# Up projections of a block as seven block products per pair of chunks, with split weights kept in HBM

## The chip, the cores and the metric

The kernel runs on one core of a Trainium2 chip. The metric is the device time of one execution in microseconds (us), the median of several runs.

## What is computed

The reference is one inference step of a one-layer decoder trunk on 2064 prompt rows (16 learned ones and 2048) and 64 sample rows (8 sequences of 8), all in float32, D = 1024 and F = 2816. Cut to what matters:

```
z = rmsnorm(x) @ w_in                                # 1024 -> 5120, five branches
a = silu(layernorm(dwconv31(za * sigmoid(zg)))) @ w_conv_out
p = (multiscale_pool(zp) @ w_pool) * pool_scale
x = x + (sigmoid(gate_a) * a + sigmoid(gate_b) * p) @ w_out
up = dwconv3(rmsnorm(x) @ w_up)                      # 1024 -> 2 x 2816
v, g = up[:F], up[F:]
x = x + (gelu(g) * v) @ w_down                       # 2816 -> 1024
y = rmsnorm(x)
```

The last rows before each convolution and pool are outputs too.

## The kernel before

The rows lie on the free axis, the channels on the 128 partitions, in chunks of 128 channels: 8 for D, 22 for F. The 2128 rows go in three blocks (708, 708 and 712 columns; the last holds the 64 sample rows at its end), and each block in two column tiles of half its width, since a PSUM region takes 512 columns.

**Products.** Every float32 operand is held as a rounded part (hi) and the rest (lo), and each product is three matmuls: lo times hi, hi times lo, hi times hi (`gemm`, matmuls at line 200). A unit is one chunk of output channels: up projections take 8 contraction chunks x 2 column tiles x 3 = 48 matmuls into one PSUM buffer of two regions. There are four such buffers in turn. `join` lets the first three units of some stages run together, chunk by chunk, as their operands appear.

**Weights.** `w_loads` fetches a unit's float32 weights (512 KB) into one of two raw tiles; `w_split` rounds them on ScalarE (line 183) and takes the rest on VectorE (line 167), into one of four places. Weights are read and split anew for each block and column tile: 416 times.

**Work beside the products.** Each unit has a post-processing step (`post`). For the up projections (`v_post`, `g_post`, `up_conv`) ScalarE scales by the last tap, VectorE adds the two other taps (line 171) and handles the sample rows apart (three small steps); the gate half then has a Gelu on ScalarE, the product with the value half on VectorE, the rounding on ScalarE and the rest on VectorE. Norms, convolution and pooling are tasks written as generators.

**Order.** One Python loop writes the instructions: it goes through the units, and after each one lets `drip` write steps of posts, weight splits and tasks, in this order of urgency, until VectorE's forecast time (`Pace`, a table of costs) is near that of TensorE. Each engine then runs its own list in order and waits by semaphores. All DMAs go through one queue, SP's, in the order written.

**Feed-forward of a block** (`FF`). Value and gate chunk f in turn, each its own unit. After a group of chunks the down projection over this group (`DN`: 8 units, each adds its result to x) is put behind the first up projections of the next group. The last block has groups of 8, 7 and 7, its first units and its last down projection go by column tile, and x stays in SBUF (`add_post`).

Of the kernel before, what the change touches and what calls it, by code (L numbers as in the profile page):

```python
# [14 lines left out]
P = 128  # L15
D = 1024
KC = D // P
F = 2816
# [33 lines left out]
RAW_BUFS = 2  # L52
F_GROUPS = (6, 5, 5, 6)
# [8 lines left out]
LAST_GROUPS = (8, 7, 7)  # L62
OWN = 4
POOL_ORDER = (1, 0, 3, 2)
BOTH, FIRST, SECOND = (0, 1), (0,), (1,)
# [3 lines left out]
class Pace:  # L69
    """A rough forecast of when each engine gets to an instruction; it only orders the work between engines."""  # L70
# [30 lines left out]
    def alloc(self, tag, bufs, ap):  # L101
        """A tile of a rotating pool waits for the last use of the tile that had its place."""
# [9 lines left out]
class Unit:  # L112
    def __init__(self, w, mm, post, needs, wait):
        self.w, self.mm, self.post, self.needs, self.wait = w, mm, post, needs, wait
        self.joined = False
# [8 lines left out]
def trunk(ctx: ExitStack, tc: tile.TileContext, A, O):  # L124
# [4 lines left out]
    mpool = ctx.enter_context(tc.tile_pool(name="mpool", bufs=2))  # L129
    ppool = ctx.enter_context(tc.tile_pool(name="ppool", bufs=4, space=bass.MemoryType.PSUM))  # L130
# [16 lines left out]
    def room(k):  # L147
        """Waits until k more tiles fit, beside a few for the work that can't wait."""
# [50 lines left out]
    def mm(out, lhsT, rhs, start, stop, rate=1.0):  # L199
        nc.tensor.matmul(out, lhsT=lhsT, rhs=rhs, start=start, stop=stop)  # L200
        pace.put("pe", size(out) * rate / 2.4 + 2.5, [out], [lhsT, rhs])
# [21 lines left out]
    def sb(ap, b, ts_):  # L223
        """The columns of a tile that belong to the column tiles ts_, in the shape of ps_of."""
# [9 lines left out]
    wq = []  # L234
    wsplits = {}
    wstate = {"load": 0, "split": 0, "done": 0}

    def w_loads():
        while wstate["load"] < min(len(wq), wstate["done"] + RAW_BUFS):
            src, n = wq[wstate["load"]][:2]  # L240
            raw = pace.alloc("raw", RAW_BUFS, wpool.tile([P, n], F32, tag="raw", name=nm("raw"), bufs=RAW_BUFS))
            load(raw, src)
            wq[wstate["load"]].append(raw)
            wstate["load"] += 1

    def w_split(i):
        while len(wq[i]) < 3:
            yield "cond", lambda: len(wq[i]) > 2
        n, raw = wq[i][1], wq[i][2]
        wh = pace.alloc("wh", W_BUFS, wpool.tile([P, n], F32R, tag="wh", name=nm("wh")))  # L250
        wl = pace.alloc("wl", W_BUFS, wpool.tile([P, n], F32R, tag="wl", name=nm("wl")))
        wq[i].append((wh, wl))
        yield "at", max(pace.ready(wh), pace.ready(raw))
        act(wh, raw, AF.Copy)
        yield at(wh)
        tt(wl, raw, wh.bitcast(F32), ALU.subtract)
        wstate["done"] += 1
        w_loads()

    def w_start(first):  # L260
        w_loads()
# [5 lines left out]
    def w_ahead(i, first):  # L267
        """Weights up to number i are split when this returns; more are under way, first is the oldest still in use."""
# [10 lines left out]
    def gemm(ps, w, pairs, rng, woff=0):  # L279
        """Products of float32 operands held as two parts each; the product of the two small parts is below float32."""  # L280
        wh, wl = w
        last = len(pairs) - 1
        for k, (xh, xl) in enumerate(pairs):
            w0 = woff + k * P
            for i, (c0, c1) in enumerate(rng):
                o = ps[:, i, : c1 - c0]
                mm(o, wl[:, w0 : w0 + P], xh[:, c0:c1], k == 0, False)
                mm(o, wh[:, w0 : w0 + P], xl[:, c0:c1], False, False)
                mm(o, wh[:, w0 : w0 + P], xh[:, c0:c1], False, k == last)
# [990 lines left out]
```

## Time and profile before

| what | value |
|---|---|
| median of 3 runs | 3006.57 us (3005.26 to 3006.57) |
| span of the profiled execution | 3004.0 us |
| TensorE busy | 2963.5 us, 18156 instructions |
| VectorE busy | 2162.5 us |
| ScalarE busy | 970.3 us |
| read from and written to HBM | 236.09 and 12.75 MB |

The page gives for the profiled execution the span from its first to its last instruction; the median lies 2.6 us above it. A row of a group reads: line, engine, operation, output<-inputs, shapes, count | busy us, mean ns of one | idle us of the engine just before, and what ended most of it. A row of waits reads: who waited <- for whom: us in total, times, longest us. A row of the timeline reads: start us, duration us, engine, line, operation, and in brackets the idle time before. A row of a stretch reads: from:to and its length, then the busy us (and the number of instructions) of PE, PEld, DVE, ACT and POOL, the granted clock, the DMA engines' busy share (of one, or of the stretch's us in its length) and GB/s; where only PE was asked for, its busy us stands alone. PE is TensorE, DVE VectorE, ACT ScalarE, SP the engine that issues the DMAs.

### The profile page before, as it was taken

How to read it: one execution, taken by the hardware profiler on the slowest of the kernel's cores; microseconds unless marked ns; L12 is line 12 of the kernel's file. 1: busy time of each engine (PE TensorE's matmuls, PEld its weight loads, DVE VectorE, ACT ScalarE, POOL GpSimd, SP SyncE). 2: the span in 40 equal slices, each digit the busy share in tenths (PEclk: the TensorE clock that was granted, in tenths of full speed). 3: DMA queues.
4: the chain of work that ended last, by engine and by line, in shares of the span. 5: the costliest groups of instructions: out<-in, count | busy, mean ns of one | idle time of the engine just before them, and what ended most of it. 6: DMA issues, size and time to landing. Idle time of an engine off the chain costs nothing.

```text
span 3004.0 us, 43514 instructions
## 1 busy us (share of the span) xinstructions
PE 2963.5 (99%) x18156; PEld 2956.5 (98%) x18156; DVE 2162.5 (72%) x2958; ACT 970.3 (32%) x1311; POOL 87.9 (3%) x185
## 2 busy tenths in 40 slices
PE   7999999999999999999999999999999999999998
PEld 7999999999999999999999999999999999999998
DVE  7999998789899856633698899986763366535356
ACT  4212234343222333522332322333352244313132
POOL 0111000010000000000010000000000000000000
PEclk9999999999999999999999999999999999999999
DMA  4211221422221223123332122222322242222223
GB/s 166 75 36 60 71 70 47 156 80 60 74 71 55 79 86 119 64 78 117 122 99 68 61 80 65 66 74 75 122 86 77 96 137 74 79 68 77 71 77 114
DMA packets 95235, 251.64 MB, mean 84 GB/s; under 512 B 22080, under 2 KB 30400, under 8 KB 95040
## 3 DMA queue, kind: packets, MB, share of 16 engines
q1 hardware_dynamic: 95040, 248.88, 25.4%
q8 instruction: 142, 2.33, 0.3%
q14 instruction: 53, 0.43, 0.0%
HBM read 236.09 MB, written 12.75 MB: 83 GB/s over the span
## 4 chain that ended last, share of the span: by engine, by line
PE 97%; DVE 2%; ACT 1%; issue 0%; DMA 0%; SPq 0%; DVEq 0%; ACTq 0%
PE ps L200 97%; DVE s L171 1%; ACT s L183 1%; DVE s L167 1%; DMA s<-in_x 0%; DVE rs L171 0%; DVE wl L167 0%; ACT wh L183 0%; DVE rs L167 0%; SPq L192 0%; DVE rs L179 0%; DVE uw L167 0%; DVE rs L177 0%; DVEq L1258 0%; ACTq L183 0%
## 5 line engine op out<-in xcount | busy, mean ns | idle before, releaser
L200 PE MATMUL ps<-s,wh 128*128 128x354 f32 (+2 forms) x11904 | 2907.9, 326 | 8.0 <-DVE s L167 7.9
L200 PEld LDWEIGHTS ps<-s,wh 128*128 128x128 f32 x11904 | 2097.9, 189 | 10.7 <-DVE s L167 10.4
L200 PE MATMUL ps<-s,wl 128*128 128x356 f32 (+2 forms) x5952 | 1944.6, 327 | 6.8 <-ACT s L183 3.7
L200 PEld LDWEIGHTS ps<-s,wl 128*128 128x128 f32 x5952 | 1122.8, 189 | 8.9 <-ACT s L183 7.3
L171 DVE SCALAR_TENSOR_TENSOR s<-s,half,s 128x708 f32<-128x708 f32 (+1 forms) x720 | 626.7, 928 | 0.0
L167 DVE TENSOR_TENSOR wl<-raw,wh 128x1024 fp32r<-128x1024 f32 (+4 forms) x416 | 476.6, 1147 | 193.2 <-ACT wh L183 190.3
L183 ACT ACTIVATE wh<-raw 128x1024 fp32r<-128x1024 f32 (+4 forms) x416 | 412.3, 994 | 550.6 <-PE ps L200 410.5
L183 ACT ACTIVATE s<-s 128x708 fp32r<-128x708 f32 (+7 forms) x424 | 296.7, 710 | 548.0 <-DVE s L171 397.1
L167 DVE TENSOR_TENSOR s<-s,s 128x708 f32<-128x708 f32 (+7 forms) x453 | 358.5, 801 | 93.6 <-ACT s L183 89.4
L171 DVE SCALAR_TENSOR_TENSOR s<-ps,cst,s 128x708 f32<-128x708 f32 (+3 forms) x276 | 254.6, 924 | 189.4 <-ACT sf L183 109.7
L183 ACT ACTIVATE s<-ps,cst 128x708 f32<-128x708 f32 (+3 forms) x138 | 113.5, 825 | 457.6 <-PE ps L200 457.6
L167 DVE TENSOR_TENSOR s<-s,ps 128x708 f32<-128x708 f32 (+3 forms) x160 | 123.1, 779 | 144.9 <-PE ps L200 144.1
L183 ACT ACTIVATE s<-ps 128x708 f32<-128x708 f32 (+3 forms) x121 | 82.5, 690 | 396.4 <-PE ps L200 396.3
L171 DVE SCALAR_TENSOR_TENSOR s<-s,s 128x708 f32<-128x708 f32 (+2 forms) x96 | 85.3, 891 | 44.0 <-ACT s L183 42.4
L171 DVE SCALAR_TENSOR_TENSOR s<-s,ps 128x708 f32<-128x708 f32 (+5 forms) x65 | 44.0, 698 | 91.2 <-PE ps L200 90.5
L171 DVE SCALAR_TENSOR_TENSOR s<-s,cst,s 128x708 f32<-128x708 f32 (+3 forms) x112 | 83.5, 767 | 27.9 <-ACT s L183 14.8
L167 DVE TENSOR_TENSOR s<-s 128x722 f32<-128x722 f32 (+7 forms) x60 | 53.2, 886 | 17.0 <-ACT s L183 15.6
L171 DVE SCALAR_TENSOR_TENSOR sc<-sa,cst,sc 128x64 f32<-128x64 f32 x232 | 47.1, 278 | 0.3
L183 ACT ACTIVATE s<-s,half 128x708 f32<-128x708 f32 (+1 forms) x48 | 46.5, 975 | 0.8
L188 POOL COPY s<-phist 128x15 f32<-128x15 f32 x24 | 12.8, 534 | 1014.8 <-ACT s L183 1007.3
L188 POOL CAST s<-hhist 128x2 fp32r<-128x2 f32 x48 | 19.2, 416 | 642.9 <-PE ps L200 555.3
L200 PEld LDWEIGHTS ps<-ones,s 128*128 128x128 f32 x144 | 18.6, 197 | 11.8 <-issue 11.7
(43 smaller groups left out, 273.4 us busy)
## 6 DMA issues: line engine op xcount, KB each, us to landing
raw<-in_w_up SPq DMA_DIRECT2D x132, 512.0 KB, 3.3
raw<-in_w_in SPq DMA_DIRECT2D x112, 512.0 KB, 3.3
raw<-in_w_out SPq DMA_DIRECT2D x40, 512.0 KB, 3.3
s<-in_x SPq DMA_DIRECT2D x40, 354.0 KB, 6.1
raw<-in_w_co SPq DMA_DIRECT2D x24, 512.0 KB, 3.3
raw<-in_w_dn SPq DMA_DIRECT2D x32, 384.0 KB, 3.1
s<-in_x SPq DMA_DIRECT2D x32, 356.0 KB, 5.9
raw<-in_w_dn SPq DMA_DIRECT2D x24, 448.0 KB, 3.4
```

The costliest lines, as they stand in the source:

```text
L167: nc.vector.tensor_tensor(out=out, in0=a, in1=b, op=op)
L171: nc.vector.scalar_tensor_tensor(out=out, in0=a, scalar=s, in1=b, op0=op0, op1=op1)
L183: nc.scalar.activation(out, a, func, **kw)
L188: nc.gpsimd.tensor_copy(out, a)
L200: nc.tensor.matmul(out, lhsT=lhsT, rhs=rhs, start=start, stop=stop)
```

## The change

**Seven products.** For chunks 2 to 21 of the last block, `pair(b, f)` replaces the units of value chunk f and gate chunk f. The two chunks, the two halves of the contraction (chunks 0 to 3 and 4 to 7) and the two column tiles make a 2 x 2 by 2 x 2 block product. Eight block products become seven, of 4 contraction chunks x 3 = 12 matmuls of 358 columns each. They go into four PSUM regions x, a, bb and d of two buffers: first x, second a, third bb, fourth onto x, fifth onto bb, sixth d, seventh onto a. ScalarE copies the first results of x, a and bb (`copy`) before the fourth, seventh and fifth product add to these regions, and copies x again after the fourth. VectorE makes the outputs by five additions of 358 columns (`after`); then `v_post` and `g_post` follow as before, from SBUF.

```diff
+            x, a, bb, d = ps1[:, 0, :n], ps1[:, 1, :n], ps2[:, 0, :n], ps2[:, 1, :n]
+            prod(x, 0, 0, b11, True)
+            c1 = copy(pq[:, :n], x)
+            yield
+            prod(a, 1, 0, mx[1], True)
+            c5 = copy(pq[:, n:], a)
+            yield
+            prod(bb, 2, 0, mx[3], True)
+            for t in older:
+                done(t)
+            pu = S(2 * n)
+            c7 = copy(pu[:, :n], bb)
+            yield
+            done(c1)
+            prod(x, 0, h, b21, False)
+            w_start(w[1])
+            uv = S(2 * n)
...
+            done(c7)
+            prod(bb, 1, h, mx[4], False)
+            w_start(w[3])
+            yield
+            prod(d, 3, 0, mx[2], True)
+            yield
+            done(c5)
...
+            prod(a, 3, h, b22, False)
+            w_start(w[3] + 1)
```

`older` are the posts that are unfinished when the pair begins; all of them are written out ahead of c7. `mixed_rows` makes the combined inputs once (four rounds, each with four subtractions of 358 columns, two roundings and two rests of 716); `first_mixed` keeps the float32 rows for it. `mixed_weights`, the last of all tasks, makes the combined weights of each pair from block 1 on: one load of value and gate chunk, four combinations and seven parts of 512 columns, each rounded, its rest taken, and both stored in HBM.

```diff
+            x0, x1 = R["xt", b][k], R["xt", b][k + KC // 2]
...
+            tt(t1, b12, b11, ALU.subtract)
+            tt(t2, b22, t1, ALU.subtract)
+            tt(t3, b22, b12, ALU.subtract)
+            tt(t4, b21, t2, ALU.subtract)
```

**Weights kept.** A weight that comes again is stored in HBM as hi and lo after its first split (1 MB), and later loaded so, with no split: 136 splits remain (40 of w_in, 8 of w_co, 8 of w_out, 44 of w_up, 4 of w_pool, 32 of w_down).

```diff
+            q.both = pace.alloc("wb", W_BUFS, wpool.tile([P, 2, q.n], F32R, tag="wb", name=nm("wb")))
+            if q.known:
+                load(q.both.bitcast(F32), known(q.key))
...
+        if q.again:
+            stores.append(i)
```

**Groups and x of the last block.** The groups are 2, 5, 5, 5 and 5 chunks in place of 8, 7 and 7. x is stored in HBM after the second norm, and each down projection but the last loads a chunk, adds and stores it again; `x_back` loads it for the last.

```diff
+PLAIN = 2
+MIX_GROUPS = (2, 5, 5, 5, 5)
...
-LAST_GROUPS = (8, 7, 7)
...
                     yield from add_post(b, c, ts_, ps, "x2n" if f1 == FC else None)
+                    if f1 < FC and b in MIXED:
+                        spill(b, c)
...
+                if b in MIXED and f >= PLAIN:
+                    pair(b, f)
```

**How instructions move.** ScalarE, up projections of the last block, before: value chunk (ps_23743), gate chunk (ps_23816), and the splits (wh) between; the last two rows are Gelu and rounding.

```order
L183 ACTIVATE s_23867<-ps_23743,cst 128x712
L183 ACTIVATE sf_23741<-ps_23743 128x8x8
L183 ACTIVATE wh_23792<-raw_23739 128x1024
L183 ACTIVATE uhist<-ps_23743 128x2
L183 ACTIVATE s_23934<-ps_23816,cst 128x712
L183 ACTIVATE sf_23814<-ps_23816 128x8x8
L183 ACTIVATE wh_23865<-raw_23809 128x1024
L183 ACTIVATE uhist<-ps_23816 128x2
L183 ACTIVATE s_23934<-s_23934 128x712
L183 ACTIVATE s_23935<-s_23867 128x712
```

ScalarE, the same place now: the post of one pair (s_22983 and s_23032 are its value and gate rows), then the copies of the next pair, whose buffers are ps_23038 (x and a) and ps_23039 (bb and d).

```order
L194 ACTIVATE s_23054<-s_22983,cst 128x712
L194 ACTIVATE sf_22899<-s_22983 128x8x8
L194 ACTIVATE uhist<-s_22983 128x2
L194 ACTIVATE s_23076<-s_23032,cst 128x712
L194 ACTIVATE sf_23015<-s_23032 128x8x8
L194 ACTIVATE uhist<-s_23032 128x2
L194 ACTIVATE s_23076<-s_23076 128x712
L194 ACTIVATE s_23077<-s_23054 128x712
L194 ACTIVATE s_23040<-ps_23038 128x358 x2
L194 ACTIVATE s_23104<-ps_23039 128x358
L194 ACTIVATE s_23120<-ps_23038 128x358
```

The splits are gone, four copies from PSUM have come, and the copies of x and a (s_23040) stand behind the Gelu and the rounding of the pair before.

TensorE, before, from one up projection to the next; the new buffer is waited for, and nothing inside a unit.

```order
L200 MATMUL ps_23743<-s_21468,wh_23512 128x358
L200 MATMUL ps_23743<-s_21467,wh_23512 128x358
L200 MATMUL ps_23816<-s_21319,wl_23586 128x358 [waits DVE_49,PE_49,Activation_49]
L200 MATMUL ps_23816<-s_21320,wh_23585 128x358
L200 MATMUL ps_23816<-s_21319,wh_23585 128x358
```

TensorE now, in the pair of ps_23038 and ps_23039: the end of the third product, the fourth onto x, and the start of the fifth onto bb.

```order
L211 MATMUL ps_23039<-s_22360,wb_23000 128x358
L211 MATMUL ps_23039<-s_22359,wb_23000 128x358
L211 MATMUL ps_23038<-s_21781,wb_22981 128x358 [waits Activation_49]
L211 MATMUL ps_23038<-s_21781,wb_22981 128x358 x2
L211 MATMUL ps_23038<-s_21789,wb_22981 128x358 x3
L211 MATMUL ps_23038<-s_21824,wb_22981 128x358 x3
L211 MATMUL ps_23038<-s_21833,wb_22981 128x358 x3
L211 MATMUL ps_23039<-s_22166,wb_22998 128x358 [waits Activation_49]
```

Inside a pair there are now waits for ScalarE, at the fourth and fifth product (and the seventh).

SP, before, in the last block: a load of weights for a down projection, sample rows in, sample rows out.

```order
L192 DMA raw_25259<-in_w_dn 128x896
L192 DMA sf_25261<-in_st_ffn 128x80
L196 DMA out_ffn_s<-sf_25194 128x80
L192 DMA raw_25329<-in_w_dn 128x896
L192 DMA sf_25334<-in_st_ffn 128x80
L196 DMA out_ffn_s<-sf_25261 128x80
```

SP now, in the first down projection of the last block: xd is x in HBM, wb the weights, keep their place in HBM.

```order
L207 DMA out_ffn_s<-sf_22452 128x80
L203 DMA s_22500<-xd_0_21998 128x712
L203 DMA wb_22515<-keep_6635 128x2x256
L203 DMA s_22517<-xd_1_22014 128x712
L203 DMA wb_22532<-keep_6684 128x2x256
L207 DMA xd_0_21998<-s_22500 128x712
L203 DMA s_22536<-xd_2_22022 128x712
L203 DMA wb_22551<-keep_6733 128x2x256
L207 DMA xd_1_22014<-s_22517 128x712
L203 DMA s_22555<-xd_3_22039 128x712
```

Between two loads of weights stand a fetch and a spill of x, and from the third fetch on each one stands behind the spill of two chunks before, which waits for that chunk's addition.

More of the change, by code (lines that the diff above doesn't have):

```diff
@@ L234, in trunk @@
     wq = []
+    kept = {}
+    stores = []
     wsplits = {}
-    wstate = {"load": 0, "split": 0, "done": 0}
-    def w_loads():
[L239 to L243, printed above, removed]
+    wstate = {"load": 0, "split": 0, "done": 0, "raws": 0, "first": 0}
@@ new lines, in known, with keep @@
+    def known(key):
+        if key[0] != "dn":
+            return kept.get(key)
+        _, c, f0, f1 = key
+        done = kept.get(("dn", c), (None, ()))
+        return done[0][:, :, f0 * P : f1 * P] if all(f in done[1] for f in range(f0, f1)) else None
+    def keep(key, n):
+        if key[0] == "dn":
+            _, c, f0, f1 = key
+            if ("dn", c) not in kept:
+                kept["dn", c] = dpool.tile([P, 2, F], F32, tag=f"keep_{len(kept)}", name=f"keep_{len(kept)}"), set()
+            kept["dn", c][1].update(range(f0, f1))
+            return known(key)
+        kept[key] = dpool.tile([P, 2, n], F32, tag=f"keep_{len(kept)}", name=f"keep_{len(kept)}")
+        return kept[key]
@@ new lines, in w_stores @@
+    def w_stores(upto):
+        while stores and stores[0] <= upto:
+            q = wq[stores.pop(0)]
+            store(keep(q.key, q.n), q.both.bitcast(F32))
+    def w_loads():
+        while wstate["load"] < min(len(wq), wstate["first"] + LEAD):
+            q = wq[wstate["load"]]
+            q.known = known(q.key) is not None
+            if not q.known and wstate["raws"] >= wstate["done"] + RAW_BUFS:
+                break
+            w_stores(wstate["load"] - W_BUFS)
+            q.both = pace.alloc("wb", W_BUFS, wpool.tile([P, 2, q.n], F32R, tag="wb", name=nm("wb")))
+            if q.known:
+                load(q.both.bitcast(F32), known(q.key))
+            else:
+                q.raw = pace.alloc("raw", RAW_BUFS, wpool.tile([P, q.n], F32, tag="raw", name=nm("raw"), bufs=RAW_BUFS))
+                load(q.raw, q.src)
+                wstate["raws"] += 1
@@ L244, in w_loads @@
             wstate["load"] += 1
     def w_split(i):
[L247 to L256, printed above, removed]
+        q = wq[i]
@@ L692, in co_post, with spill, fetch, x_back @@
         R.setdefault(("m", b), []).append((hi, lo))
+    def spill(b, c):
+        if ("xd", b, c) not in R:
+            R["xd", b, c] = dpool.tile([P, WIDTHS[b]], F32, tag=f"xd_{b}_{c}", name=f"xd_{b}_{c}")
+        store(R["xd", b, c], R.pop(("x1", b, c)))
+    def fetch(b, c):
+        x = R["x1", b, c] = S(WIDTHS[b])
+        load(x, R["xd", b, c])
+    def x_back(b):
+        for c in range(KC):
+            yield from room(1)
+            fetch(b, c)
     def x_again(b):
```

250 lines of the change are left out of this document (221 added, 29 removed).

## Prediction

> **What bounds the kernel now.** I read the page first: busy times, then the chain that ended last.
>
> ```profile
> span 3004.0 us, 43514 instructions
> PE 2963.5 (99%) x18156; PEld 2956.5 (98%) x18156; DVE 2162.5 (72%) x2958; ACT 970.3 (32%) x1311; POOL 87.9 (3%) x185
> PE 97%; DVE 2%; ACT 1%; issue 0%; DMA 0%; SPq 0%; DVEq 0%; ACTq 0%
> ```
>
> TensorE is busy 99% of the span and carries 97% of the chain. Time can be won only by giving it fewer matmuls, and is lost wherever it is made to wait. So the second view is TensorE's own waits, the third its busy time by stretch, in the up projections of the last block.
>
> ```profile
> PE ps L200 <- DVE s L167: 19.3, 7, 9.6
> PE ps L200 <- DVE rs L171: 7.1, 5, 2.0
> PE ps L200 <- ACT s L183: 3.7, 3, 1.8
> PE ps L200 <- DVE s L171: 3.0, 4, 1.1
> 2600.00:2700.00 100.00, 100.00 (x615) 100.00 (x614) 39.72 (x50) 23.56 (x33) 0.00 (x0) 1.00 0.24 73
> 2700.00:2800.00 100.00, 100.00 (x611) 100.00 (x610) 58.62 (x87) 34.12 (x59) 0.00 (x0) 1.00 0.25 73
> ```
>
> All waits together are 33 us, none longer than 9.6. In the stretch that the change rewrites TensorE never waits; 1226 matmuls in 200 us are 163.1 ns each. There every new wait costs its full length.
>
> **Matmuls removed.** A pair of chunks took 2 x 8 x 2 x 3 = 96 matmuls, 15.66 us. Seven products of 4 x 3 take 84, 13.70 us. Twenty pairs: 240 x 163.1 ns = 39.1 us less. A product is 12 matmuls, 1.96 us. The regrouped down projections keep their matmul count.
>
> **Splits removed, mixed weights added.** 280 of 416 splits go. They cost VectorE and ScalarE, not the bound:
>
> ```profile
> L167 DVE TENSOR_TENSOR wl<-raw,wh 128x1024 fp32r<-128x1024 f32 (+4 forms) x416 | 476.6, 1147 | 193.2 <-ACT wh L183 190.3
> L167 DVE TENSOR_TENSOR wl<-raw,wh 128x512 fp32r<-128x512 f32 x12 | 8.2, 686 | 11.1 <-ACT wh L183 11.1
> ```
>
> VectorE saves 280 x 1.147 = 321 us and gets 20 x 11 steps of 512 columns, 220 x 0.686 = 151 us, at the lowest priority. The cover is TensorE's own work: I cost both at nothing. The bounds are -3 and +3 us, the waits from 2400 to 2500 us, round the last block's second norm, won or had once more (SP now meets stores that wait for VectorE ahead of loads):
>
> ```profile
> PE ps L200 <- DVE s L171: 1.5, 2, 1.1
> PE ps L200 <- DVE s L167: 1.3, 1, 1.3
> PE ps L200 <- DVE rs L171: 0.5, 1, 0.5
> ```
>
> Without that cover the last mixed weights would be late at the first pair.
>
> **The copies inside a pair: the main term.** The fourth product adds onto the region that held the first (x), so it waits until ScalarE has copied x. That copy stands on ScalarE behind the whole post-processing of the pair before, as the order rows show. How long that post-processing takes is read from a chunk's in the trace, first ScalarE, then VectorE:
>
> ```profile
> 2611.92 0.86 ACT L183 ACTIVATE s<-ps,cst 128x712 f32<-128x712 f32 x1 [4.74 <-PE ps L200]
> 2615.84 0.80 ACT L183 ACTIVATE s<-s 128x712 f32<-128x712 f32 x1 [0.76 <-DVE s L171]
> 2617.61 0.80 ACT L183 ACTIVATE s<-s 128x712 fp32r<-128x712 f32 x1 [0.97 <-DVE s L167]
> 2618.32 1.05 ACT L183 ACTIVATE wh<-raw 128x1024 fp32r<-128x1024 f32 x1
> ...
> 2612.92 1.96 DVE L171 SCALAR_TENSOR_TENSOR s<-ps,cst,s 128x712 f32<-128x712 f32 x2 [3.88 <-ACT sf L183]
> 2614.91 0.26 DVE L177 TENSOR_SCALAR s<-sf,cst 128x64 f32<-128x64 f32 x1
> 2615.20 0.61 DVE L171 SCALAR_TENSOR_TENSOR s<-sf,cst,s 128x64 f32<-128x64 f32 x2
> 2616.68 0.90 DVE L167 TENSOR_TENSOR s<-s,s 128x712 f32<-128x712 f32 x1 [0.87 <-ACT s L183]
> 2618.44 0.90 DVE L167 TENSOR_TENSOR s<-s,s 128x712 fp32r<-128x712 f32 x1 [0.87 <-ACT s L183]
> ```
>
> For the steps that this stretch lacks, the nearest rows are these; the third shows that taps which read SBUF take about as long as those from PSUM above (0.96 against 1.96 / 2), the fourth that a matmul's result lies 0.16 us (326 less 163 ns) behind the start of the next:
>
> ```profile
> L167 DVE TENSOR_TENSOR s<-s,ps 128x356 f32<-128x356 f32 x32 | 16.6, 522 | 17.0 <-PE ps L200 16.7
> L183 ACT ACTIVATE s<-ps 128x356 f32<-128x356 f32 x11 | 5.0, 457 | 10.5 <-PE ps L200 10.5
> L171 DVE SCALAR_TENSOR_TENSOR s<-s,cst,s 128x712 f32<-128x712 f32 x16 | 15.3, 956 | 8.9 <-DMA s<-in_x 8.9
> L200 PE MATMUL ps<-s,wh 128*128 128x354 f32 (+2 forms) x11904 | 2907.9, 326 | 8.0 <-DVE s L167 7.9
> ```
>
> Let S be the start of the next pair's first product. Four of the five combining additions need only the sixth product, visible at S - 1.8; 4 x 0.52 us end at S + 0.3, and the fifth, after the seventh product, at S + 0.8. Then ScalarE's scaling and sample copy, 1.0 us to VectorE's start (2611.92 to 2612.92): S + 1.8. Value taps and sample taps 2.9 us: S + 4.7. Gate taps to Gelu 2.9 us (2612.92 to 2615.84): S + 7.6. Gelu, product, start of the rounding 1.8 us (to 2617.61): S + 9.4. Next ScalarE instruction 0.7 us later: S + 10.1. The copy, 0.46 us: S + 10.55. TensorE has done three products at S + 5.88. It waits 4.67 us.
>
> This hits each pair that directly follows a pair. With groups of 2, 5, 5, 5, 5, and the pending down projection put behind the first pair of a group, these are 4 + 4 + 4 + 3 = 15: 70.0 us. Bounds per wait: 4.2 (the additions back to back hide 0.4) and 5.2 (the sample rows land 0.5 late, as SP now loads them behind three weights).
>
> **The clock after such a wait.** The trace has one wait of this size:
>
> ```profile
> 492.37 0.96 PE L200 MATMUL ps<-s,wh 128*128 128x354 f32 x2 [4.59 <-DVE s L167]
> 495.70 0.32 PE L200 MATMUL ps<-s,wl 128*128 128x354 f32 x1
> 493.00:494.00 1.00, 1.00 (x5) 0.50 0.34 135
> 498.00:499.00 1.00, 1.00 (x8) 1.00 0.00 0
> ```
>
> After 4.59 us of waiting the granted clock was 0.50, and 11 matmuls from 492.37 to 495.70 took 3.33 us in place of 1.79: 1.54 us more. One case proves no rule, so I take it for half of 18 places (15 waits and three below): 13.9 us, bounds 0 and 27.7.
>
> The Trainium skill, "TensorE: Matmul & The Clock Gate", section "What's actually happening", says that the clock halves after an idle window of about 3.4 us that runs freely. The 4.59 us row agrees. If each wait held such a window, every one would pay, which is rival 1.
>
> **The first pair.** It needs the mixed rows: four rounds on VectorE, each four subtractions of 358 columns and two rests of 716, between the posts that were there before.
>
> ```profile
> L167 DVE TENSOR_TENSOR s<-s,s 128x712 f32<-128x712 f32 x50 | 43.9, 894 | 4.8 <-ACT s L183 4.3
> 2487.66 1.18 DVE L167 TENSOR_TENSOR s<-s,s 128x356 fp32r<-128x356 f32 x2
> 2492.45 1.06 ACT L183 ACTIVATE wh<-raw 128x1024 fp32r<-128x1024 f32 x1 [4.18 <-PE ps L200]
> 2494.68 1.21 DVE L171 SCALAR_TENSOR_TENSOR s<-ps,cst,s 128x356 f32<-128x356 f32 x2
> 2500.54 0.53 DVE L167 TENSOR_TENSOR s<-s,s 128x356 fp32r<-128x356 f32 x1 [0.57 <-ACT s L183]
> ```
>
> A round is 4 x 0.52 + 2 x 0.89 = 3.9 us. The norm ends at 2488.8, three rounds at 2500.5. The posts of value and gate (2494.68 to 2501.07) cost 6.4 us, of the second value chunk 2 us: 2509. The last plain gate's post is 6.4 us (2612.92 to 2619.34): 2515.3. The fourth round needs 2.9 us until its first rest: 2518. TensorE ends the half-tile units at 2492.4, the last plain unit (48 matmuls, 7.8 us) at 2500.2, and the first product with three quarters of the second at 2503.7. It waits 14 us; this place held 1.3 us of waits already, so +13. Bounds 6 (posts packed without their pauses) and 16.
>
> **The first down projection, two chunks deep.** Eight units of 12 matmuls, 15.7 us. VectorE does the first addition after the first pair's post (the rest ends at S + 11.1, the addition at S + 12.0), and the fifth unit, at S + 7.84, needs the buffer: 4.1 us late. Behind that stands the DMA queue:
>
> ```profile
> 12.00:14.00 2.00, 0.97 (x4) 1.00 1.06 372
> raw<-in_w_up SPq DMA_DIRECT2D x132, 512.0 KB, 3.3
> ```
>
> Fetches and spills of x and weights are 8 x (0.365 + 0.365 + 0.262) = 7.9 MB, the next pair's first weight 1.05 MB. At the 372 GB/s of a stretch in which the queue was full, 9.0 MB take 24.1 us, 8.4 beyond the 15.7 of the products; the pair's next two weights, behind the last fetches, make it some 12. Bounds 4 (only VectorE) and 15. In the five-chunk groups a unit takes 4.9 us and moves 1.4 MB (3.7 us): no cost.
>
> **The last down projection.** The last pair's rest is ready at S + 11.1; three joined half units with four finished chunks cover 36 matmuls, 5.9 us. Before, seven chunks covered 8.8 us and the post was shorter. +5, bounds 4 and 6.
>
> **Weights within the pairs.** Each is now up to 1.05 MB with four buffers, so the next pair's first weight is asked for after the fourth product, three products (5.9 us) ahead of its use. No row has 1 MB; 512 KB land in 3.3 us, so 3.3 to 6.6. With the added half MB at 372 GB/s, 1.4 us, it is 4.7: no cost; the upper end is a rival. Ahead of it on SP stand two stores of sample rows, which wait for ScalarE until about S + 3.2, long before the fourth product ends.
>
> The Trainium skill, "DMA: Bandwidth & Descriptors", section "Anatomy of one DMA — SWDGE (gpsimd) path", gives 2.0 us plus bytes at 436 GB/s, by which 1.05 MB would be 4.4 us and the sum unchanged; no run here shows that size.
>
> **Sum.** -39.1 + 70.0 + 13.9 + 13 + 12 + 5 = +74.8 us on a span of 3004.0. The median of the runs, 3006.57, is 2.6 above the span, which I leave as it is: 3081.4, say 3081 us.
>
> **Rivals.**
> 1. The clock halves after every long wait: 27.7 for 13.9, 3095 us. For it: the one row of 4.59 us. Against: the wait may straddle two windows of whatever decides. Chance 0.25.
> 2. It never does: 3067 us. Against: the same row. Chance 0.15.
> 3. Weights come late in every pair: 6.6 us to land and 0.3 to issue against 5.9 is 1.0 x 15, 3096 us. Against: the slope of the queue at 372 GB/s. Chance 0.07.
> 4. Faster: the copy isn't late. If ScalarE reaches the copy of x before S + 5.4, the 15 waits and their clock go; -39.1 + 13 + 12 + 5 + 2 leaves -7, 2999 us, and 2967 if the other three are hidden too. That is decided by the length of the post. Against: the gate part alone took 6.5 us from scaling to the end of rounding (2611.92 to 2618.41). Chance 0.05.
> 5. Within 0.2% (6 us, about what measurement can tell here): the value part of the post hides wholly, each wait is 1.8 us, 27 in all, and the rest falls to its lower bounds: -39 + 27 + 6 + 4 + 4 = +2, 3008 us. Chance 0.03.
> That the change doesn't do what it says is excluded by the order: 240 matmuls fewer stand on TensorE.
>
> **Numbers.** The forecast has 0.45, with its own range 3055 to 3105. The low end takes waits of 4.2, no clock loss and lower bounds elsewhere: -39 + 63 + 6 + 4 + 4 = +38, 3045; the high end waits of 5.2, every clock loss and upper bounds: -39 + 78 + 28 + 16 + 15 + 6 = +104, 3110. Rivals 1 to 3 lie inside; I give 3042 to 3110. Slower 0.92, same 0.03, faster 0.05.
>
> **What would show it.** In the profile after: 240 matmuls fewer; TensorE waiting for ScalarE on ps some 15 times for 4 to 5 us, at the start of the fourth product; clocks of about 0.5 in slices behind such waits; a wait of about 13 us near 2500 us; pairs 18 to 20 us apart. Pairs 13.7 us apart, or ScalarE's copies finished ahead of the third product, would prove me wrong.

## The result and the profile after

| | before | after |
|---|---|---|
| median | 3006.57 us | 3171.14 us (3164.82 to 3177.41) |
| ratio | | 1.0548 (95%: 1.0530 to 1.0567) |
| span of the profiled execution | 3004.0 us | 3175.6 us |

The change makes the kernel 164.6 us slower at the median, 171.6 us in the profiled executions. The direction was forecast, the size was not: 3081, with 3110 as the upper end. The four executions after took 3165 us twice and 3177 us twice, at mean granted clocks of 0.970 and 0.966, and the profiled one is the longest of them. First the page after: busy times and the chain that ended last.

```profile
span 3175.6 us, 44290 instructions
PE 3000.8 (94%) x17916; PEld 2976.3 (94%) x17916; DVE 2072.6 (65%) x3046; ACT 829.4 (26%) x1259; POOL 99.0 (3%) x201
PE 86%; DVE 8%; ACT 3%; DMA 2%; issue 1%; SPq 0%; DVEq 0%; ACTq 0%
```

TensorE has 240 instructions fewer and is busy 37 us longer: many run at a lower clock, as the slices further down show. Its share of the chain falls from 97% to 86%. Its waits after:

```profile
PE ps L211 <- ACT s L194: 109.5, 38, 8.8
PE ps L211 <- DVE s L178: 37.2, 15, 10.3
PE ps L211 <- DVE rs L182: 11.2, 7, 2.1
PE ps L211 <- DMA wb<-keep: 7.0, 6, 2.7
```

The first row was 3.7 us in 3 waits before. TensorE's timeline shows what it is; the rows are, in order, the first pair, the fifth unit of the first down projection, two pairs, and the last down projection.

```profile
2553.59 0.67 PE L211 MATMUL ps<-s,wb 128*128 128x358 f32 x1 [8.81 <-ACT s L194]
...
2578.95 5.72 PE L211 MATMUL ps<-s,wb 128*128 128x356 f32 x24 [4.11 <-DVE s L178]
...
2645.00 3.95 PE L211 MATMUL ps<-s,wb 128*128 128x358 f32 x12 [4.52 <-ACT s L194]
2649.87 14.19 PE L211 MATMUL ps<-s,wb 128*128 128x358 f32 x72 [0.92 <-ACT s L194]
2668.59 3.63 PE L211 MATMUL ps<-s,wb 128*128 128x358 f32 x12 [4.52 <-ACT s L194]
2673.14 12.07 PE L211 MATMUL ps<-s,wb 128*128 128x358 f32 x72 [0.92 <-ACT s L194]
...
3122.24 0.66 PE L211 MATMUL ps<-s,wb 128*128 128x356 f32 x1 [4.23 <-ACT s L194]
```

A pair is 12 matmuls behind a wait of 4.5 us (the fourth product), then a second wait of 0.92 us, then 72 matmuls (the fifth, sixth and seventh product and three of the next pair). The 12 take 3.63 to 3.95 us in place of 1.96. ScalarE at the same place, from the Gelu of the pair before to the copies of this one:

```profile
2665.62 0.80 ACT L194 ACTIVATE s<-s 128x712 f32<-128x712 f32 x1 [4.61 <-DVE s L182]
2667.38 0.80 ACT L194 ACTIVATE s<-s 128x712 fp32r<-128x712 f32 x1 [0.96 <-DVE s L178]
2668.08 0.45 ACT L194 ACTIVATE s<-ps 128x358 f32<-128x358 f32 x1
2672.26 1.19 ACT L194 ACTIVATE s<-ps 128x358 f32<-128x358 f32 x3 [3.72 <-PE ps L211]
```

The copy of x follows the rounding, ends at 2668.53, and the fourth product starts at 2668.59: the forecast wait. (This pair's first product starts near S = 2658.2, the end of the 72 matmuls less three products of 1.96 us; Gelu, rounding and end of the copy then lie at S + 7.4, 9.2 and 10.3, where the prediction had 7.6, 9.4 and 10.55.) The three other copies wait 3.72 us more, until the fourth product has ended, and run together; the fifth product waits for the copy of bb, which is among them. Nothing in the data needs that: the copy of a reads a region that the fourth product doesn't write. It shares its PSUM buffer with x.

The last block isn't the only place. Around the second norm of block 1, where TensorE never waited before (1400 to 1600 us held 200.00 us of its work), stands now:

```profile
1488.93 1.47 PE L211 MATMUL ps<-ones,s 128*128 128x1 f32 x12 [2.88 <-DVE s L178]
1492.47 2.93 PE L211 MATMUL ps<-cst,rs 128*128 128x128 f32 x12 [2.07 <-DVE rs L182]
1505.73 2.69 PE L211 MATMUL ps<-ones,s 128*128 128x1 f32 x12 [10.33 <-DVE s L178]
1510.49 2.93 PE L211 MATMUL ps<-cst,rs 128*128 128x128 f32 x12 [2.07 <-DVE rs L182]
1518.39 0.67 PE L211 MATMUL ps<-s,wb 128*128 128x356 f32 x1 [4.98 <-ACT s L194]
```

To follow this through the kernels I use marks: VectorE's first step on the root of a norm (rs<-ps), which each kernel has once per norm or half. Before:

```profile
1448.25 0.17 DVE L177 TENSOR_SCALAR rs<-ps 128x6 f32<-128x6 f32 x1 [0.34 <-PE ps L200]
2470.66 0.16 DVE L177 TENSOR_SCALAR rs<-ps 128x3 f32<-128x3 f32 x1 [2.57 <-PE ps L200]
```

After:

```profile
1508.45 0.17 DVE L188 TENSOR_SCALAR rs<-ps 128x6 f32<-128x6 f32 x1 [2.06 <-PE ps L211]
2508.38 0.16 DVE L188 TENSOR_SCALAR rs<-ps 128x3 f32<-128x3 f32 x1 [0.98 <-PE ps L211]
```

The first mark is block 2's first norm. Before, it was done while TensorE still had block 1's output projections to do, and block 2's first projections then filled block 1's second norm; now it comes 60 us later, and TensorE has nothing there. The second mark is the second half of the last block's second norm, just ahead of its feed-forward: 37.7 us late. From it to the end before takes 533.3 us, after 667.2, 133.9 more.

### The profile page after: what moved, and what is told of

Its sections match the earlier page's. It is cut to its first block, busy times and chain, and to the rows that moved or that the text cites. A ratio compares the mean times of both kernels' runs of the same rounds, so it can differ in the third digit from the quotient of the medians.

```text
span 3175.6 us, 44290 instructions
## 1 busy us (share of the span) xinstructions
PE 3000.8 (94%) x17916; PEld 2976.3 (94%) x17916; DVE 2072.6 (65%) x3046; ACT 829.4 (26%) x1259; POOL 99.0 (3%) x201
## 4 chain that ended last, share of the span: by engine, by line
PE 86%; DVE 8%; ACT 3%; DMA 2%; issue 1%; SPq 0%; DVEq 0%; ACTq 0%
PE ps L211 86%; DVE s L182 4%; DVE s L178 3%; ACT s L194 2%; DMA wb<-keep 1%; DMA s<-in_x 0%; DVE s L188 0%; DMA s<-xd 0%; DMA sf<-in_st_ffn 0%; DVE rs L182 0%; DVE wb L178 0%; DVE rs L178 0%; DMA keep<-s 0%; DVE rs L190 0%; ACT wb L194 0%
## 5 line engine op out<-in xcount | busy, mean ns | idle before, releaser
L211 PE MATMUL ps<-s,wb 128*128 128x356 f32 (+2 forms) x17616 | 2962.7, 330 | 130.9 <-ACT s L194 109.5
L211 PEld LDWEIGHTS ps<-s,wb 128*128 128x128 f32 x17616 | 2934.8, 192 | 152.4 <-ACT s L194 122.6
L194 ACT ACTIVATE s<-s 128x708 fp32r<-128x708 f32 (+9 forms) x452 | 316.2, 709 | 769.6 <-DVE s L182 422.2
L178 DVE TENSOR_TENSOR s<-s,s 128x708 f32<-128x708 f32 (+10 forms) x533 | 405.4, 773 | 138.9 <-ACT s L194 121.1
L178 DVE TENSOR_TENSOR s<-s,ps 128x708 f32<-128x708 f32 (+4 forms) x236 | 168.4, 723 | 465.7 <-PE ps L211 365.1
L194 ACT ACTIVATE s<-ps 128x358 f32<-128x358 f32 (+4 forms) x201 | 116.0, 601 | 650.8 <-PE ps L211 614.2
L182 DVE SCALAR_TENSOR_TENSOR s<-ps,cst,s 128x708 f32<-128x708 f32 (+2 forms) x196 | 177.9, 910 | 87.0 <-ACT s L194 83.3
L178 DVE TENSOR_TENSOR wb<-raw,wb 128x1024 fp32r<-128x1024 f32 (+3 forms) x136 | 153.0, 1127 | 48.2 <-ACT wb L194 47.4
L182 DVE SCALAR_TENSOR_TENSOR s<-s,cst,s 128x712 f32<-128x712 f32 (+3 forms) x192 | 160.2, 847 | 36.7 <-ACT s L194 35.3
L194 ACT ACTIVATE wb<-raw 128x1024 fp32r<-128x1024 f32 (+3 forms) x136 | 132.2, 977 | 166.4 <-PE ps L211 125.0
```

What stands on the lines that cost most here:

```text
L178: nc.vector.tensor_tensor(out=out, in0=a, in1=b, op=op)
L182: nc.vector.scalar_tensor_tensor(out=out, in0=a, scalar=s, in1=b, op0=op0, op1=op1)
L194: nc.scalar.activation(out, a, func, **kw)
```

## The experiments

Times are medians, with the ratio to the kernel before where it matters. The marks are read as above; "block 2's middle" is its convolution's norm.

| kernel | first norm, block 2 | block 2's middle | last second norm | from there to the end |
|---|---|---|---|---|
| before | 1448.25 | 2137.95 | 2470.66 | 533.3 |
| after | 1508.45 | 2176.99 | 2508.38 | 667.2 |
| copies first | 1506.74 | 2175.39 | 2508.05 | 534.1 |
| copies first, three plain chunks | 1507.14 | 2175.79 | 2505.17 | 509.2 |
| only kept weights | 1479.96 | 2156.16 | 2484.81 | 535.8 |
| the same, w_out not kept | 1440.61 | 2137.53 | 2466.78 | 535.4 |
| combined weights paused | 1487.24 | 2152.65 | 2502.17 | 654.4 |
| first norm's sum early | 1371.76 | 2160.89 | 2500.80 | 663.5 |

### Inside the pairs

**Copies first.** The copies of x, a and bb are written right behind the third product, ahead of the posts of the pair before.

```diff
-            for t in older:
-                done(t)
             pu = S(2 * n)
             c7 = copy(pu[:, :n], bb)
+            for t in (c1, c5, c7):
+                done(t)
             yield
...
             prod(bb, 1, h, mx[4], False)
+            for t in older:
+                done(t)
```

> The copies of the first three products (x, a, bb) stand on ScalarE ahead of the post-processing of the pair before, right behind the third product. Theory A (the copies are late because they stand behind that post-processing): the 15 waits of 4.5 us and the 15 of 0.92 us go, 82 us, and with them the halved clock behind them, 2 to 4.3 us each, 30 to 64 us: 3171 - 112 to 146 = 3025 to 3059 us, pairs 13.7 to 14.2 us apart. Rival B (weights of 1 MB or free PSUM buffers bind a pair next): a new wait of 2 to 3 us per pair takes the place, 3070 to 3105 us, and TensorE waits on wb or for VectorE in each pair. Rival C (something else on ScalarE or VectorE holds the pairs at 18 to 20 us): within 10 us of 3171.

3048.46 us, as theory A has it. A stretch of pairs there, TensorE's row of after first:

```profile
2601.00:3120.00 519.00, 434.80 (x2323) 422.68 (x2321) 203.76 (x346) 100.04 (x226) 0.00 (x0) 0.88 0.62 208
```

and with the copies first:

```profile
2600.00:2979.00 379.00, 375.94 (x2293) 375.07 (x2292) 195.50 (x332) 97.92 (x218) 0.00 (x0) 1.00 0.80 282
```

163.9 ns a matmul, clock 1.00, no waits to speak of. After, nearly the same work (30 matmuls more) has 84.2 us of waits and 434.8 - 2323 x 0.1639 = 54 us of lost clock. The marks ahead of the feed-forward stay: what is lost there is another matter.

**Matmuls in place of the wait.**

```diff
             yield
+            for j in range(0 if f in (2, 3, 8, 13, 18) else 26):
+                mm(d, wq[w[0]].both[:, 0, :P], b11[0][0], True, True)
             done(c1)
```

> Before the fourth product of the 15 pairs that follow a pair, 26 more matmuls (4.2 us at 163 ns) go into the region d, whose contents the sixth product later overwrites: TensorE is busy in place of waiting, the copies come when they came. Theory A (the clock is halved because TensorE idles 4.5 us): full clock behind, 2 to 4.3 us less per pair, 30 to 64 us in all, 3107 to 3141 us, though more is done. Rival B (the slow products behind the wait have another cause, such as ScalarE's or VectorE's reads of PSUM, or the load of the chip): no change, 3165 to 3177 us, the first products behind the extra matmuls still at half speed.

3130.97 us, 40 us less, though 390 matmuls more are done:

```profile
2623.41 2.24 PE L211 MATMUL ps<-s,wb 128*128 128x358 f32 x12 [0.25 <-ACT s L194]
2626.57 16.35 PE L211 MATMUL ps<-s,wb 128*128 128x358 f32 x98 [0.92 <-ACT s L194]
```

The fourth product takes 2.24 us, and 98 matmuls behind it 16.35 (167 ns each): full speed. So it is TensorE's idling that halves the clock, and not what ScalarE or VectorE do meanwhile. The 0.92 us stayed.

**Sixth product before the fourth.** The copies are written out first, then the sixth product, then the fourth.

```diff
+            for t in (c1, c5, c7):
+                done(t)
+            prod(d, 3, 0, mx[2], True)
             yield
-            done(c1)
             prod(x, 0, h, b21, False)
...
-            prod(d, 3, 0, mx[2], True)
```

> The sixth product, which needs no copy, comes ahead of the fourth, and all three copies are written before it, still behind the post-processing of the pair before. Theory A (the wait is 4.5 us because only three products of 1.96 us lie between a pair's start and the first need of a copy, and the clock halves only behind a wait of that length): the wait falls to 4.5 - 2.0 = 2.6 us, the second wait of 0.92 goes, the clock stays at 1.00: 15 x (1.96 + 0.92 + 2 to 4.3) = 73 to 108 us less, 3063 to 3098 us. Rival B (the clock halves behind shorter waits too): 15 x 2.9 = 43 us less, 3128 us. Rival C (the weight of the sixth product, asked for last of the four, isn't there so early): waits on wb of some 1 to 2 us per pair, 15 to 30 us above A.

3163.83 us, none of the three theories: the sixth product itself, which needs no copy, waits.

```profile
2625.79 16.02 PE L211 MATMUL ps<-s,wb 128*128 128x358 f32 x84 [4.94 <-ACT s L194]
2647.05 15.64 PE L211 MATMUL ps<-s,wb 128*128 128x358 f32 x84 [5.23 <-ACT s L194]
```

Its region d lies in one buffer with bb, and the copy of bb that stands before it in the program reads that buffer. So in this kernel a dependency is on the whole buffer, not on its region. The same explains the 0.92 us: the copy of a, written behind the fourth product, has to wait for that product's writes to x.

**Sixth product fourth.** Now all four first writes come ahead of the copies that share their buffers.

```diff
+            prod(d, 3, 0, mx[2], True)
             for t in older:
                 done(t)
             pu = S(2 * n)
             c7 = copy(pu[:, :n], bb)
+            for t in (c1, c5, c7):
+                done(t)
             yield
-            done(c1)
             prod(x, 0, h, b21, False)
...
-            prod(d, 3, 0, mx[2], True)
```

> The sixth product comes fourth, straight behind the third, and only behind it stand the copies of a PSUM buffer that it shares (the run with the sixth product ahead of the fourth had it wait for the copy of bb, which reads the same buffer). All copies are still behind the post-processing of the pair before. Theory A (a dependency is on a whole PSUM buffer, not on its region, so that the sixth product waited there; the wait is set by the post-processing, and the clock halves only behind waits of over 3.4 us or so): the wait is 4.5 + 0.45 (copies of x and a, one buffer) - 1.96 = 3.0 us, the second wait of 0.92 goes, the clock stays: 15 x (1.5 + 0.9 + 2 to 4.3) = 66 to 100 us less, 3071 to 3105 us. Rival B (clock halves behind 3.0 us as well): 15 x 2.4 = 36 us less, 3135 us. Rival C (the sixth product still waits for ScalarE): within 10 us of 3164.

3078.21 us, in theory A's range, and the sixth product waits for no copy. But the waits are shorter than forecast, and for weights:

```profile
2634.84 14.14 PE L211 MATMUL ps<-s,wb 128*128 128x358 f32 x84 [1.02 <-DMA wb<-keep]
2649.89 14.39 PE L211 MATMUL ps<-s,wb 128*128 128x358 f32 x84 [0.91 <-DMA wb<-keep]
```

ScalarE's order had changed more than was meant: the copies of x and a slipped ahead of the rounding (x2 here), some 2 us earlier.

```profile
2650.49 0.80 ACT L194 ACTIVATE s<-s 128x712 f32<-128x712 f32 x1 [4.51 <-DVE s L182]
2651.19 0.81 ACT L194 ACTIVATE s<-ps 128x358 f32<-128x358 f32 x2
2652.25 0.80 ACT L194 ACTIVATE s<-s 128x712 fp32r<-128x712 f32 x1 [0.25 <-DVE s L178]
```

Whether a wait of 3.0 us halves the clock was therefore not tested here; the kernel after has a wait near it (2.68 us), which is read with the clock below.

**Copies first, three plain chunks, groups of 5, 5, 6 and 6.**

```diff
-PLAIN = 2
-MIX_GROUPS = (2, 5, 5, 5, 5)
+PLAIN = 3
+MIX_GROUPS = (5, 5, 6, 6)
```

> The copies first, as in the run of 3048 us, and in addition chunk 2 as plain products (19 pairs in place of 20) and groups of 5, 5, 6 and 6 chunks. Theory A (the first pair's wait of 8.8 us for the combined rows, the first down projection's waits, 4.1 + 0.5 + 0.3 + 2.6 + 0.5 + 0.9 = 8.8 us, and the last one's, 2.9 + 4.1 + 0.5 = 7.5 us, come from work that is too short to cover them): the first two go with some 2 us each of halved clock, the third loses about 3 us, and 12 matmuls more cost 2.0 us: 3048 - 23 = 3025 us (3018 to 3034). Rival B (mixed rows on VectorE are late whatever covers them, or deeper groups run out of room in SBUF): 3040 to 3055 us.

3018.38 us: the waits of the first pair and of the first down projection are gone. From the last second norm to the end it takes 509.2 us, 24 less than before: with its waits covered the seven products do pay, by 24 of the 37 us that 19 pairs remove. All of it and more is lost ahead of that mark.

### Ahead of the last feed-forward

**Only kept weights.** No pairs, no combined rows or weights.

```diff
-MIXED = (NBLK - 1,)
+MIXED = ()
+LAST_GROUPS = (8, 7, 7)
...
-    add_task(("mw",), mixed_weights(), mark["PG", 1])
```

> Only the half of the change that keeps split weights in HBM: no seven products, no combined rows or weights, groups of 8, 7 and 7 chunks and x in SBUF as before. Theory A (of the 37 us by which the last block's feed-forward starts late, the kept weights cost some 7, round 640 us where their stores begin, and the combined weights' stores the other 30): 3007 to 3016 us. Rival B (the kept weights, as 1 MB loads in place of 512 KB and with their stores, cost the 37 us): 3036 to 3046 us, with the waits of 10.3, 5.0 and 2.9 us near 1490 to 1520 us still there. Rival C (fewer splits free VectorE and ScalarE, and waits go): 2985 to 3003 us.

3020.94 us (1.0048, 1.0033 to 1.0063), between A and B: kept weights cost 14 of the 38 us and, if the two add up, combined weights 24.

**Combined weights paused** from block 1's output projections to the start of its feed-forward.

```diff
+        if mark["WO", 1] <= now["i"] < mark["FF", 1] + 2:
+            rest = [t for t in rest if t.name[0] != "mw"]
```

> The task that makes the combined weights rests from the output projections of block 1 to the second unit of its feed-forward, so that none of its loads and stores stand on SP among the loads of x for block 2's first norm. Theory A (these stores hold up the loads of x, block 2's first projections start late, and TensorE has nothing to fill block 1's second norm with): the waits between 1486 and 1520 us go, 25 to 31 us, 3140 to 3146 us. Rival B (the 1 MB loads of kept weights, which also stand there and wait for buffers, hold up the loads of x): the waits stay, 3165 to 3177 us.

3161.72 us, between both. The marks say why: by block 2's middle 24.3 us are won, at the last second norm 6.2 are left. The rest of the combined weights now meets block 2's output projections, where TensorE waits for kept w_out:

```profile
2435.56 21.25 PE L211 MATMUL ps<-s,wb 128*128 128x356 f32 x120 [4.23 <-DMA wb<-keep]
2461.53 6.24 PE L211 MATMUL ps<-s,wb 128*128 128x356 f32 x24 [4.16 <-DMA wb<-keep]
2489.72 10.74 PE L211 MATMUL ps<-s,wb 128*128 128x356 f32 x54 [5.66 <-DMA wb<-keep]
```

**Stores on a queue of their own.**

```diff
-            store(keep(q.key, q.n), q.both.bitcast(F32))
+            nc.gpsimd.dma_start(out=keep(q.key, q.n), in_=q.both.bitcast(F32))
```

and so for the stores of combined weights.

> The stores of kept and of combined weights are issued by GpSimd on a queue of its own, and no longer stand on SP among the loads; nothing else is changed. Theory A (the block 2 feed-forward starts 38 us late because loads stand on SP behind stores that wait for ScalarE, VectorE or room in the queue): 25 to 38 us less, 3133 to 3146 us, with no waits of 10.3, 5.0 and 2.9 us at 1486 to 1520 us and none of 5.6 us at 642 us. Rival B (what holds up the loads is the amount of data that moves, or the 1 MB loads): 3165 to 3177 us. Rival C (GpSimd's small copies of histories then stand behind stores, and the norms wait for them): slower than 3177 us.

3169.76 us: rival B. Waits of 10.33, 2.93 and 4.97 us stood where they had stood. My theory that loads stand on SP behind stores fell.

**The ordering's DMA clock without stores.** `Pace` forecasts when a loaded tile can be used, and stores take time of that forecast.

```diff
-        pace.put("dma", size(src) * P * 4 / 340.0, [], [src], late=2000.0)
+        pace.put("out", size(src) * P * 4 / 340.0, [], [src], late=2000.0)
```

> Only the table by which the Python loop orders the work is changed: stores no longer take time of the DMA clock that says from when a loaded tile can be used (every DMA is still on SP, and every instruction is still there, some at another place). Theory A (the added stores push that clock ahead, so that the steps of block 2's first norm, which wait for loads of x, are written late into the engines' lists; this, and not SP's queue, which the run with a queue of its own left at 3170 us, makes the last block's feed-forward start 38 us late): 25 to 38 us less, 3133 to 3146 us, and most of the waits near 642 us and from 1486 to 1520 us gone. Rival B (the loads of x really land late, because of the 1 MB weights and the stores, however the steps are ordered): the steps then wait on the engines, 3160 to 3180 us.

3155.90 us, 15 less and 11 of them ahead of the last feed-forward (2497.42): between the two. The same edit upon the faster version (copies first, three plain chunks), and upon kept weights alone:

> The copies first, three plain chunks and groups of 5, 5, 6 and 6, as in the run of 3018 us, and stores that take no time of the ordering's DMA clock. Theory A (the clock of the ordering costs 25 to 38 us, independently of the pairs): 2980 to 2993 us, faster than the kernel before by 0.5 to 0.9%. Rival B (loads really late): 3010 to 3020 us.

3011.11 us (1.0013, 1.0004 to 1.0022): rival B's range, 7 us less than without.

> Only kept weights, no seven products, as in the run of 3021 us, and stores that take no time of the ordering's DMA clock. Theory A (the 14 us by which kept weights are slower come from the order that this clock makes): 3004 to 3012 us. Rival B (they come from the 1 MB loads or from stores that stand on SP among the loads): 3016 to 3024 us.

3019.43 us: rival B.

**Loads of x on a queue of their own**, in VectorE's old order, then with that clock, upon the faster version, and upon kept weights alone.

```diff
-        load(x, A["x"][c, :, COL0[b] + c0 : COL0[b] + c1])
+        nc.gpsimd.dma_start(out=x, in_=src)
```

> Loads of whole rows of x (for the first norms of blocks 1 and 2 and for the residual) are issued by GpSimd on another queue; nothing else is changed, and VectorE's list is the same row for row. Theory A (on SP these loads stand behind loads of kept weights, which wait until TensorE has left one of the four places): the waits from 1486 to 1520 us (2.9 + 2.1 + 10.3 + 2.1 + 5.0 us and the clock behind them) go, 20 to 31 us less, 3140 to 3151 us. Rival B (the steps that use x are written late into the engines' lists by the ordering, whenever the loads land): 3160 to 3177 us. Rival C (GpSimd issues them later than SP, behind its small copies): slower than 3177 us.

3168.50 us: rival B.

> Loads of x on GpSimd's queue, and stores that take no time of the ordering's DMA clock. Theory A (loads behind kept weights, and an ordering that writes their users late, each hold a part): 25 to 38 us less than 3171, 3133 to 3146 us. Rival B (both leave it, and there is a third cause): as the run with the clock alone, 3150 to 3160 us.

3170.75 us, no gain, and neither theory has it.

> The version of 3011 us (copies first, three plain chunks, groups of 5, 5, 6 and 6, the ordering's clock without stores) with the loads of x on GpSimd's queue. Theory A: 15 to 25 us less, 2986 to 2996 us, faster than before by 0.3 to 0.7%. Rival B (x isn't what is late): 3005 to 3015 us.

3018.33 us, 7 us more than without.

> Only kept weights, no seven products (3021 us), with the loads of x on GpSimd's queue. Theory A (with no combined weights about, the loads of x are late only because they stand on SP behind loads of kept weights that wait for TensorE): some 7 to 11 of the 14 us go, 3010 to 3014 us. Rival B (they are late for another reason): 3017 to 3024 us.

3027.67 us, 7 us more than without. The loads of x are not late for their queue.

**The first norm's sum early.** The sum of squares for block 2's first norm may be written 16 units earlier.

```diff
-mark["WO", b] if b else 2)
+mark["WO", b] - 16 if b else 2)
```

> The sum of squares for the first norm of block 2 may be written 16 units earlier (from among the convolution's output projections of block 1); nothing else is changed. Theory A (TensorE waits from 1486 to 1520 us because this sum comes late, so that block 2's first projections can't fill block 1's second norm): those waits shrink by 15 to 25 of their 23 us, with their clock, 3146 to 3156 us or less. Rival B (the normed rows of block 2 are late too, for room in SBUF or for VectorE, whenever the sum is done): 3162 to 3177 us.

3164.02 us at the end, in rival B's range, but 16.1 us won by block 2's middle, as theory A had it; 8.5 are then lost again at the same place as with the pause, on waits for kept w_out of 4.0 and 2.7 us. With the faster version:

> The version of 3011 us (copies first, three plain chunks, groups of 5, 5, 6 and 6, the ordering's clock without stores) with that sum of squares 16 units earlier. Theory A: 10 to 20 us less, 2991 to 3001 us, faster than before by 0.2 to 0.5%. Rival B: 3008 to 3016 us.

3003.62 us, ratio 0.9991 (0.9982 to 1.0000). It is the best that was run, and no measurable gain on the kernel before.

**w_out not kept**, in the kernel with kept weights alone.

```diff
-            q.again = all(k in last for k in parts_)
+            q.again = all(k in last for k in parts_) and q.key[0] != "out"
```

> Only kept weights, no seven products (3021 us), and of these w_out alone isn't kept: it is loaded and split anew each time as before (512 KB in place of 1 MB per unit of the output projections, 32 splits more). Theory A (the kept loads of w_out, 1 MB for units that take 3.9 or 7.8 us, hold up what stands behind them on SP: the first weights of the up projections at 642 us, x at 1490 us): 7 to 14 us less, 3007 to 3014 us, with the waits of 5.6 us at 642 us and of 1.3 to 2.1 us round 1490 to 1500 us gone or shorter. Rival B (they are late for another reason): 3017 to 3024 us.

3005.28 us, ratio 0.9995 (0.9986 to 1.0005): theory A, and a little more. All marks are back where they were before or ahead. The stretch of block 0's output projections over the second column tile, with w_out kept (in this order: length, the five engines, clock, DMA share, GB/s):

```profile
560.00:600.00 40.00, 39.89 (x250) 39.82 (x250) 18.16 (x37) 10.41 (x18) 2.18 (x6) 1.00 0.91 329
```

and not kept:

```profile
560.00:600.00 40.00, 40.00 (x252) 40.00 (x251) 24.48 (x42) 15.85 (x23) 1.90 (x6) 1.00 0.42 135
```

A unit of one column tile there takes 24 matmuls, 3.9 us, and kept w_out brings 1 MB for each. In these 40 us six such loads (median 8.0 us to land) and five stores of 1 MB are issued; without the keeping there are eleven raw loads of 512 KB (3.3 us) and no store. Loads and stores together fill the DMA engines to 0.91; which of the two matters was not separated. That the first weights of the up projections and the next x then come late is the reading that fits. About half of the loss is there by block 0's second norm (633.96 us against 626.44), the rest comes round 1490 us, behind block 1's output projections, whose units take 7.8 us.

## Why the prediction was right in direction and wrong in size

By its own steps, in the profiled executions; the parts add up to 3175.6 - 3004.0 = 171.6 us, 97 more than the 74.8 forecast.

| step | forecast | measured |
|---|---|---|
| matmuls removed | -39.1 | -39.1 (240 instructions) |
| waits for the copy of x, 15 | 70.0 | 67.4 (4.04 to 4.63 each) |
| second wait in a pair | none | 14.7 (16 of 0.92) |
| clock behind the pairs' waits | 11.6 of 13.9 | 54 |
| first pair, first and last down projection, with clock | 13 + 12 + 5 + 2.3 | 36.9 (what is left of the 133.9) |
| splits, kept and combined weights | 0 (-3 to 3) | 37.7 |

**Right.** The main term, its mechanism and its price: 4.67 us forecast, 4.52 measured, because the copy of x stands behind the whole post-processing. Putting the copies first took it away. Of the 36.9 us the waits themselves are 9.1 at the first pair (13 forecast), 8.3 in the first down projection (12) and 4.9 in the last (5); most of the rest is slower matmuls.

**The step that failed: "I cost both at nothing."** The prediction took the removed splits and the added loads and stores as covered by TensorE's work, with bounds read at the last block's second norm alone. It looked at how long VectorE is busy, not at which steps a late transfer holds. The term measured 37.7 us. 14 of them came from kept weights, and there from w_out alone (shown: without it 3005 us). The other 24 came with the combined weights. That they delay block 2's first norm is shown by the pause (24.3 us by block 2's middle) and by the early sum (16.1); how is not: another queue for the stores, or for x, changed nothing, the ordering's forecast only a part. A rival that the runs leave standing is the amount of data itself: from 1420 to 1480 us the DMA engines were busy 0.51 of the time at 183 GB/s before and 0.93 at 345 GB/s after, and a load of block 2's rows took a median of 9.7 us to land in place of 5.1. VectorE is a less likely one, since it was busy 35 us of these 60 before and 26 after. What was won came half to three quarters undone at block 2's output projections, where kept w_out is waited for. Leaving w_out out of the keeping together with the combined weights was not tried.

**The clock, a term of the wrong size.** The prediction took 1.54 us for half of the places; its rival 1 took 1.54 for all of them, 3095 us. Each of the 15 waits was followed by half speed, so the rival was right in that, and each cost 54 / 15 = 3.6 us. Against the 11.6 forecast that is 42 us, the largest part of the miss. The one row that the prediction had, 1.54 us, came from a half clock of 3.4 us; behind these waits it lasted 3.4 us three times, 6.8 twice and 10.2 ten times. All its changes in this trace lie multiples of 3.41 us apart. Cut into such steps (length, TensorE's busy time, clock, DMA share, GB/s), two pairs and the shortest of the 15 waits (4.04 us, until 2766.03) look like this:

```profile
2640.97:2644.38 3.41, 0.00 (x0) 1.00 0.80 281
2644.38:2647.79 3.41, 2.79 (x9) 0.50 0.08 31
2647.79:2651.21 3.42, 2.50 (x8) 0.50 0.37 74
2651.21:2654.62 3.41, 3.41 (x13) 0.50 0.56 233
2654.62:2658.04 3.42, 3.42 (x23) 1.00 0.48 165
...
2664.86:2668.27 3.41, 0.00 (x0) 1.00 0.85 305
2668.27:2671.69 3.42, 3.10 (x10) 0.50 0.01 2
2671.69:2675.10 3.41, 2.49 (x15) 1.00 0.52 154
...
2760.43:2763.85 3.42, 1.57 (x10) 1.00 0.47 133
2763.85:2767.26 3.41, 1.23 (x7) 1.00 0.63 264
2767.26:2770.67 3.41, 2.49 (x9) 0.50 0.21 34
```

In the first pair three steps at half follow the step that was all waiting: the first still holds the last 0.62 us of the long wait, the second the 0.92 us of the second wait, and behind the third, which is full of work, the clock is back. In the second pair the step at half holds only 0.32 us of waiting, and the clock is back behind it; the second wait comes later and doesn't lower it. In the third case no step is all waiting: the 4.04 us lie across two, and the clock stayed behind 1.85 us of waiting and fell behind 2.18. That is why none of the 15 escaped: a wait of 4.5 us, wherever it falls among steps of 3.41, leaves at least 2.25 us in one of them. The wait of 2.68 us in the first down projection (until 2592.52), all within one step, halved the clock for 3.4 us too. The Trainium skill, "TensorE: Matmul & The Clock Gate", section "What's actually happening", says that the gate looks at free-running windows of about 3.4 us, goes to half after an idle one and back after a busy one. The trace agrees on the length and on the way back; on the way down it differs if idle means idle throughout, since here 2.18 us of waiting within a window were enough.

**The second wait, not foreseen.** The rows on how instructions move show the fifth product's wait, but the prediction priced only the fourth's, as if a copy depended on its region alone. It depends on its buffer. Beside its own 14.7 us it keeps the clock down: with the sixth product ahead of the fourth there is no second wait, and no half clock in the pairs was longer than 6.8 us, though the waits there were over 4.9.

**The range.** Its upper end, 3110, took every clock loss at 27.7 us, nothing ahead of the last block and no second wait. The clock behind the 15 waits passed its bound by 31 us (54 for 23), and the two others came to 38 and 15; smaller waits than the bound gave some 15 us back.

## What to carry to other kernels

When an engine with an in-order list gets a short step that TensorE waits for, write the step ahead of the long work that already stands there; it was worth 123 us here, while a saving of 39 us was the aim. Count regions of one PSUM buffer as one for dependencies, and price a wait of over 4 us with nearly twice its length (4.5 us cost 3.6 more here), since the clock falls behind it. Before intermediate results are kept in memory, compare bytes per unit with the unit's time at every place that will load them: w_out's 1 MB for units of 3.9 and 7.8 us cost 14 us, and the same keeping elsewhere nothing.

## What the runs showed of the hardware

The granted clock moved in steps of 3.41 us: it fell behind a step with 2.18 us of waiting and not behind one with 1.85, and at half speed a wait of 0.92 us within a step put off its return by another step, while 0.32 us didn't. And a load of 1 MB took 5.4 us to land, a store of 1 MB 6.3 (medians, after; 512 KB of raw weights took 3.3 before and 5.9 after, among the added traffic).

```profile
wb<-keep SPq DMA_DIRECT2D x228, 1024.0 KB, 5.4
keep<-wb SPq DMA_DIRECT2D x100, 1024.0 KB, 6.3
raw<-in_w_up SPq DMA_DIRECT2D x84, 512.0 KB, 5.9
```

The prediction's cost for 1 MB was 4.7 us, with 3.3 to 6.6 as bounds; from 2600 to 3100 us, where the pairs are, the median was 4.9. In the pairs as they were ordered this hid; where the sixth product came fourth it became a wait of 1.0 us per pair.
